# Down projections of a two-layer decoder trunk: four of eleven pairs of k-tiles by seven block products with summed blocks in place of eight products

## The chip, the cores and the metric

The kernel runs on one core of one Trainium2 chip. The metric is the device time of one execution in microseconds: the median of three runs is 652.33 us (651.77 to 652.62). The profile is one more execution, taken with the hardware profiler, and has its own time.

The engines are named as the profile names them: PE multiplies matrices, PEld is PE's loading of the stationary operand, DVE is the vector engine (VectorE), ACT the scalar engine (ScalarE), POOL is GpSimd, and SP issues the DMA transfers of the weights.

## The reference

The input is 256 tokens of width 1024. Two layers follow each other, each a mixer and a feed-forward part; the change is in the feed-forward parts alone:

```python
D_MODEL, SEQ, DEPTH = 1024, 256, 2
D_FF = -(-8 * D_MODEL // (3 * 256)) * 256        # 2816

def rmsnorm(x, g):
    y = x * lax.rsqrt(jnp.mean(x * x, axis=-1, keepdims=True) + NORM_EPS)
    return y * g

def swiglu(h, w_gate, w_up, w_down):
    return (jax.nn.silu(h @ w_gate) * (h @ w_up)) @ w_down

for layer in range(DEPTH):
    x = x + mixer(rmsnorm(x, norm_mix[layer]))   # even: two attention groups, odd: sparse attention
    x = x + swiglu(rmsnorm(x, norm_ffn[layer]), ffn_w_gate[layer], ffn_w_up[layer], ffn_w_down[layer])
return rmsnorm(x, norm_final)
```

All of it is float32. The down projection is the product of the units, `silu(gate) * up`, a matrix of 256 tokens by 2816, with `w_down`, 2816 by 1024.

## The kernel before

**How a float32 product is made.** Each operand is split in two: a `hi` part, the value rounded to the matrix engine's `float32r` type (a copy on ACT), and a `lo` part, the rest (a subtraction on DVE). A product is then three matmuls into one bank of PSUM (function `mm3`, lines 363 to 365): hi by hi, hi by lo, lo by hi. The gate and up projections (lines 503 and 505) have a form of their own, in which one matmul of 512 columns takes both parts of the activations and one of 256 columns takes the low part of the weights.

**The weight stream.** The class `Weights` walks a list of weight tiles in the order of their use. A tile is 128 partitions by up to 1024 columns, 512 KB. `load` (line 95) issues its transfer on SP into one of four raw buffers, `prepare` makes `w_hi` on ACT (line 111) and `w_lo` on DVE (line 114), each in a ring of seven buffers. `next` hands out the next tile and first prepares the tiles up to six ahead. So there are three releases: a raw buffer is free for the next transfer when DVE has made its `w_lo`; a `w_hi` or `w_lo` buffer is free for the tile seven further on when PE has done the last matmul that reads it.

**The order on an engine.** Each engine executes its own list strictly in order and waits at an instruction until its semaphores are reached; PE alone loads stationary operands ahead. A scheduler made the lists when the program was built, from the order in which the code records operations; nothing is reordered on the chip.

**The feed-forward part** (function `ffn`) has two stages.

- *Gate and up*, eleven chunks of 256 of the 2816 columns. A chunk takes two weight tiles for gate (banks `ps_g`, two of the four banks with the tag `mm`) and two for up (banks `ps_u`, the two banks with the tag `s`). Then come, for each of its two groups of 128 columns, an ACT copy and a DVE sum out of the bank (lines 514 and 518), a scaling, the Silu and the product `hn` (lines 515, 516, 519), a tile of 128 units by 256 tokens. `split` (line 247) makes its `hT_hi` on ACT and `hT_lo` on DVE. The units stand with the units on the partitions, and so are the stationary operand of the next stage.
- *Down*, function `residual`. The 2816 units are 22 k-tiles of 128, so eleven pairs. The 1024 columns of the result are two halves `h` of 512, the 256 tokens two halves `t` of 128: four blocks, each with one of the four `mm` banks, `ps_out`. For each k-tile, one weight tile (128 units by 1024 columns) is taken, and each of the four blocks gets its three matmuls: 12 matmuls of 512 columns. The last three k-tiles are held back and taken block by block, so that a block is complete early: DVE adds it, times the token's `rs`, to the residual stream `x` (line 448), and the next norm begins (line 281), or in the last layer the final norm (lines 330 to 353).

## Time and profile before

| what | value |
|---|---|
| median of 3 runs | 652.33 us (651.77 to 652.62) |
| the profiled execution, its own time | 652.22 us |
| its span, first to last instruction | 650.4 us |
| granted TensorE clock, mean | 0.997 |
| PE busy | 638.9 us, 98% of the span |
| PEld busy | 537.5 us, 83% |
| DVE busy | 478.9 us, 74% |
| ACT busy | 403.0 us, 62% |
| DMA of the weights | 107.79 MB on SP's queue, 49.3% of 16 engines' span |
| down stage of the first layer, first to last matmul's start | 261.34 to 322.43 us |
| down stage of the second layer, first to last matmul's start | 583.33 to 643.19 us |

How to read it: times are counted in us from the start of the span. The profiled execution's own time is 1.8 us longer than its span. A row of a timeline has the start, the length, the engine, the line of the kernel, the operation with its output and inputs, and in brackets how long the engine was idle before and what ended that. A row of the groups has, after the bar, the busy time in us and the mean length of one instruction in ns, and then the idle time before the group. Matmuls of one row follow each other before the previous one has ended, so the distance of two starts, not the length of one, is what a matmul takes.

### The profile page before, as it was taken

Reading aid. Unit: us, or ns where it says so; the run is one execution under the profiler, and the core shown is the slowest. Engines: PE = TensorE matmul, PEld = TensorE weight load, DVE = VectorE, ACT = ScalarE, POOL = GpSimd, SP = SyncE. Lnnn points to the kernel's source line nnn. Section 1 sums busy time; section 2 is a strip of 40 time slices with the busy share of each in tenths; the row PEclk is TensorE's granted clock in tenths of the full one; section 3 lists DMA queues with packets and bytes.
Section 4 is the critical chain, followed back from the end, with each engine's and each line's share of the span. In section 5 each row is a group of like instructions: output and inputs, shape, how many; then the busy total and the mean of one; then the engine's idle time right before and its main releaser. Section 6 shows DMA issues by size and latency. Waiting matters only on the chain.

```text
span 650.4 us, 10025 instructions
## 1 busy us (share of the span) xinstructions
PE 638.9 (98%) x3521; PEld 537.5 (83%) x3521; DVE 478.9 (74%) x1116; ACT 403.0 (62%) x809; POOL 11.0 (2%) x26
## 2 busy tenths in 40 slices
PE   8999999999999999999999999999999999999995
PEld 5978888888888888888888877776888888888884
DVE  6999976678867677544589889797887777765424
ACT  6685748558665665433377597787676665564314
POOL 2000000100000000000000000000000000000000
PEclk9999999999999999999999999999999999999998
DMA  8834354218755655564186511402286555556501
GB/s 302 295 128 153 98 172 154 97 53 287 244 194 194 193 187 190 183 194 151 49 328 234 188 67 56 171 34 93 85 283 234 190 187 187 183 185 210 191 14 66
DMA packets 31729, 109.02 MB, mean 168 GB/s; under 512 B 3648, under 2 KB 3904, under 8 KB 31424
## 3 DMA queue, kind: packets, MB, share of 16 engines
q1 hardware_dynamic: 31104, 107.79, 49.3%
q10 hardware_dynamic: 576, 0.59, 0.3%
q8 instruction: 28, 0.46, 0.3%
q14 instruction: 21, 0.17, 0.1%
HBM read 107.32 MB, written 1.05 MB: 167 GB/s over the span
## 4 chain that ended last, share of the span: by engine, by line
PE 88%; ACT 4%; DVE 4%; DMA 2%; issue 1%; SPq 0%; POOL 0%; ACTq 0%; DVEq 0%
PE ps_g L503 12%; PE ps_u L503 12%; PE ps_out L364 8%; PE ps_out L365 8%; PE ps_out L363 8%; PE ps_u L505 6%; PE ps_g L505 6%; PE ps_in L364 5%; PE ps_in L365 5%; PE ps_in L363 5%; PE pt_p L998 2%; PE ps_o L1014 2%; PE ps_s L978 1%; DVE w_lo L114 1%; ACT e L466 1%
## 5 line engine op out<-in xcount | busy, mean ns | idle before, releaser
L114 DVE TENSOR_TENSOR w_lo<-w_raw,w_hi 128x1024 fp32r<-128x1024 f32 (+5 forms) x200 | 231.5, 1179 | 112.6 <-ACT w_hi L111 67.7
L111 ACT ACTIVATE w_hi<-w_raw 128x1024 fp32r<-128x1024 f32 (+5 forms) x200 | 203.4, 1025 | 135.5 <-PE ps_out L365 53.4
L503 PE MATMUL ps_u<-aW,w_hi 128*128 128x512 f32 x352 | 84.9, 391 | 0.0
L503 PE MATMUL ps_g<-aW,w_hi 128*128 128x512 f32 x352 | 84.5, 391 | 0.0
L364 PE MATMUL ps_in<-w_lo,aW 128*128 128x512 f32 (+5 forms) x208 | 77.2, 371 | 0.1
L363 PE MATMUL ps_in<-w_hi,aW 128*128 128x512 f32 (+5 forms) x208 | 76.8, 370 | 0.1
L365 PE MATMUL ps_in<-w_hi,aW 128*128 128x512 f32 (+5 forms) x208 | 75.5, 363 | 0.0
L503 PEld LDWEIGHTS ps_g<-aW,w_hi 128*128 128x128 f32 x352 | 64.6, 188 | 13.1 <-DVE aW L247 0.7
L503 PEld LDWEIGHTS ps_u<-aW,w_hi 128*128 128x128 f32 x352 | 64.4, 188 | 12.2
L364 PE MATMUL ps_out<-w_lo,hT_hi 128*128 128x512 f32 (+1 forms) x176 | 68.3, 388 | 0.0
L363 PE MATMUL ps_out<-w_hi,hT_hi 128*128 128x512 f32 (+1 forms) x176 | 68.3, 388 | 0.0
L365 PE MATMUL ps_out<-w_hi,hT_lo 128*128 128x512 f32 (+1 forms) x176 | 68.3, 388 | 0.0
L505 PEld LDWEIGHTS ps_u<-aW,w_lo 128*128 128x128 f32 x352 | 45.4, 191 | 1.9
L505 PEld LDWEIGHTS ps_g<-aW,w_lo 128*128 128x128 f32 x352 | 45.4, 191 | 1.9
L505 PE MATMUL ps_g<-aW,w_lo 128*128 128x256 f32 x352 | 46.0, 283 | 0.0
L505 PE MATMUL ps_u<-aW,w_lo 128*128 128x256 f32 x352 | 46.0, 283 | 0.0
L466 ACT ACTIVATE e<-e,bias 128x128 f32<-128x128 f32 (+1 forms) x96 | 42.4, 446 | 1.3 <-DVE bias L465 0.9
L364 PEld LDWEIGHTS ps_in<-w_lo,aW 128*128 128x128 f32 x208 | 39.3, 189 | 4.6 <-issue 0.5
L363 PEld LDWEIGHTS ps_in<-w_hi,aW 128*128 128x128 f32 x208 | 39.2, 189 | 4.7 <-ACT w_hi L111 0.3
L365 PEld LDWEIGHTS ps_in<-w_hi,aW 128*128 128x128 f32 x208 | 39.2, 188 | 4.6 <-issue 0.5
L365 PEld LDWEIGHTS ps_out<-w_hi,hT_lo 128*128 128x128 f32 x176 | 33.1, 188 | 6.8
L363 PEld LDWEIGHTS ps_out<-w_hi,hT_hi 128*128 128x128 f32 x176 | 33.1, 188 | 6.7
(237 smaller groups left out, 874.7 us busy)
## 6 DMA issues: line engine op xcount, KB each, us to landing
w_raw<-in_w SPq DMA_DIRECT2D x176, 512.0 KB, 3.8
w_raw<-in_w SPq DMA_DIRECT2D x8, 384.0 KB, 4.5
gain<-in_vec SPq DMA_DIRECT2D x4, 512.0 KB, 5.4
cw<-in_cw SPq DMA_DIRECT2D x2, 1024.0 KB, 7.0
w_raw<-in_w SPq DMA_DIRECT2D x4, 416.0 KB, 5.2
w_raw<-in_w SPq DMA_DIRECT2D x4, 328.0 KB, 5.1
w_raw<-in_w SPq DMA_DIRECT2D x4, 304.0 KB, 2.7
x<-in_x SPq DMA_DIRECT2D x4, 256.0 KB, 5.0
```

Of the source, the lines that this page charges most:

```text
L111: act = nc.scalar.activation(hi[:, :n], raw[:, :n], AF.Copy)
L114: sub = nc.vector.tensor_sub(lo[:, :n], raw[:, :n], hi[:, :n])
L363: TE.matmul(ps, act[0][:, k], wh, start=start, stop=False, skip_group_check=skip),
L364: TE.matmul(ps, act[0][:, k], wl, start=False, stop=False, skip_group_check=skip),
L365: TE.matmul(ps, act[1][:, k], wh, start=False, stop=stop, skip_group_check=skip),
L466: return low, A.activation(e, e, AF.Exp, scale=-1.0, bias=bias, accum_out=den)
L503: TE.matmul(dst[f], wt[0][:, i, f * P : (f + 1) * P], wide[:, k].rearrange("p z q -> p (z q)"), start=k == 0, stop=False)
L505: TE.matmul(dst[f][:, :T], wt[1][:, i, f * P : (f + 1) * P], wide[:, k, 0], start=False, stop=k == KD - 1)
L978: mmi = TE.matmul(sb[:, i], qS[t][:, h], kz[:, par, :, :ns], start=z == 0, stop=z == 1)
L998: TE.transpose(pt[:, i, b, st], e[:, i, b, st * P : (st + 1) * P], ident)
L1014: pin(TE.matmul(ob[64 * par : 64 * par + 64], vv[:, st, c : c + 64], pTs[par][:, b, st].rearrange("p j c -> p (j c)"), start=False, stop=l ...
```

## The change

The down projection of a pair of k-tiles is a product of 2 by 2 blocks: units of k-tile 2g and 2g+1, each for the token halves 0 and 1 (a11 and a21 of the first k-tile, a12 and a22 of the second), and weights with the two column halves (b11 and b12 of the first k-tile, b21 and b22 of the second). It takes eight block products, and each is three matmuls. The change computes it for the pairs 1, 3, 5 and 7 with seven:

- sums of units: S1 = a21 + a22, S2 = S1 - a11, S3 = a11 - a21, S4 = a12 - S2
- sums of weights: T1 = b12 - b11, T2 = b22 - T1, T3 = b22 - b12, T4 = b21 - T2
- products: P1 = a11 b11, P2 = a12 b21, P3 = S4 b22, P4 = a22 T4, P5 = S1 T1, P6 = S2 T2, P7 = S3 T3
- results: block (0,0) is P1 + P2, block (0,1) is P1 + P6 + P5 + P3, block (1,0) is P1 + P6 + P7 + P4, block (1,1) is P1 + P6 + P7 + P5

P2, P3 and P4 go to the banks `ps_out` of their blocks. P1, P5, P6 and P7 are accumulated over the four pairs in four banks more (`ps_p1`, `ps_p6` with the tag `s`, `ps_p5`, `ps_p7` with the tag `tp`), and are combined once, after the last of the four pairs: an ACT copy and six DVE instructions, which add them to `x`.

The sums of weights are made on DVE in float32 from two raw tiles (`pair`), and split like any weight (`halves`). Seven blocks of 512 columns are split for a pair, T1 to T4, b11, b21 and b22, where four were; b12 is not needed by itself. The split of the sums stands in two pairs of buffers, and for the second and later pairs it is recorded after the matmuls of the pair before (`close`). The sums of units are made on DVE behind the second `hn` of the chunk (`seven_units`) and are split too; the units of a22 and a12 are split as before, a21 is not split by itself. The other seven pairs, and all that stands outside the feed-forward part, have the same instructions in the same order as before.

```diff
--- before.py
+++ after.py
@@ -30,6 +30,7 @@
 OD_CHUNKS = [304, 256, 512, 512, 512, 512]
 FF_CHUNKS = [256] * 11
 WCOLS = 1024
+FAST = (1, 3, 5, 7)
 
 
 def in_tiles(chunks):
...
@@ -100,6 +104,11 @@
         nc = self.tc.nc
         while len(self.ready) < min(upto, len(self.queue)):
             i = len(self.ready)
+            if i in self.pairs:
+                if i + 2 > upto:
+                    break
+                self.pair(i)
+                continue
             self.load(i + 1)
             raw = self.raw[i]
             self.raw[i] = None
@@ -115,6 +124,58 @@
                 self.parts.append((act, sub))
             self.ready.append((hi[:, :n].rearrange("p (k c) -> p k c", k=kk), lo[:, :n].rearrange("p (k c) -> p k c", k=kk)))
 
+    def halves(self, hi, lo, src):
+        act = self.tc.nc.scalar.activation(hi, src, AF.Copy)
+        return act, self.tc.nc.vector.tensor_sub(lo, src, hi)
+
+    def pair(self, i):
+
+        V = self.tc.nc.vector
+        self.load(i + 2)
+        a, b = self.raw[i : i + 2]
+        self.raw[i : i + 2] = [None] * 2
+        sums = [self.sums.tile([P, WCOLS], F32, tag="ts", bufs=2, name="w_sum") for _ in range(2)]
+        h = slice(0, 512), slice(512, 1024)
+        got = {}
+        for n, (names, src) in enumerate((((("b11",), a), (("b21", "b22"), b)))):
+            hi = self.pool.tile([P, WCOLS], F32R, tag="hi", bufs=self.bufs[1], name="w_hi")
+            lo = self.pool.tile([P, WCOLS], F32R, tag="lo", bufs=self.bufs[1], name="w_lo")
+            c = slice(0, 512 * len(names))
+            self.parts.append(self.halves(hi[:, c], lo[:, c], src[:, c]))
+            for j, name in enumerate(names):
+                got[name] = (hi[:, h[j]], lo[:, h[j]])
+        V.tensor_sub(sums[0][:, h[0]], a[:, h[1]], a[:, h[0]])
+        V.tensor_sub(sums[0][:, h[1]], b[:, h[1]], a[:, h[1]])
+        V.tensor_sub(sums[1][:, h[0]], b[:, h[1]], sums[0][:, h[0]])
+        V.tensor_sub(sums[1][:, h[1]], b[:, h[0]], sums[1][:, h[0]])
+        self.ready += [got, None]
+        if self.open is None:
+            self.open = (got, sums)
+            self.close()
+        else:
+            self.open = (got, sums)
+
+    def close(self):
+
+        if self.open:
+            got, sums = self.open
+            for j, names in enumerate((("t1", "t3"), ("t2", "t4"))):
+                hi = self.sums.tile([P, WCOLS], F32R, tag="thi", bufs=2, name="w_shi")
+                lo = self.sums.tile([P, WCOLS], F32R, tag="tlo", bufs=2, name="w_slo")
+                self.halves(hi, lo, sums[j])
+                for n, name in enumerate(names):
+                    c = slice(512 * n, 512 * n + 512)
+                    got[name] = (hi[:, c], lo[:, c])
+            self.open = ()
+
...
@@ -379,7 +440,7 @@
                 nm.finish()
         return ps
 
-    def residual(act, nk, tail, nxt, rs=None, amid=None, gate=(), hold=False):
+    def residual(act, nk, tail, nxt, rs=None, amid=None, fast=(), seven=None, gate=(), hold=False):
 
         ps = [[mm_bank("ps_out") for _ in range(2)] for _ in range(NT)]
         inorder = amid is not None and not hold
@@ -389,11 +450,17 @@
             skip = isinstance(nxt, Final) and (t, h) == (NT - 1, 1)
             return mm3(ps[t][h], act[t], k, wt[0][:, 0, c], wt[1][:, 0, c], k == 0, k == nk - 1 - skip * tail, skip)
 
-        for k in range(nk - tail):
+        k = 0
+        while k < nk - tail:
+            if k in fast:
+                seven(ps, k)
+                k += 2
+                continue
             wt = W.next()
             for t in range(NT):
                 for h in range(2):
                     one(t, h, k, wt)
+            k += 1
         last = [W.next(hold=tail) for _ in range(tail)]
         if amid and not hold:
             order = [(t, h, 0, tail) for t, h in ((0, 0), (0, 1), (1, 0), (1, 1))]
@@ -469,8 +536,80 @@
         wide, rs = nm.wide, nm.rs
         nxt = Final() if goff == V_FIN else Norm(goff)
         with tc.tile_pool(name="ffn", bufs=1, side="left", reuse_waits="tile") as fp:
-            hh = fp.tile([P, KF, T], F32R, tag="hh", name="hT_hi")
-            hl = fp.tile([P, KF, T], F32R, tag="hl", name="hT_lo")
+            at, sums_at, o = {}, {}, 0
+            for k in range(0, KF, 2):
+                if k // 2 in FAST:
+                    at[0, k], at[0, k + 1], at[1, k + 1], sums_at[k] = o, o + P, o + 2 * P, o + 3 * P
+                    o += 7 * P
+                else:
+                    for i in range(2):
+                        for t in range(NT):
+                            at[t, k + i] = o + (NT * i + t) * P
+                    o += 4 * P
+            hh = fp.tile([P, o], F32R, tag="hh", name="hT_hi")
+            hl = fp.tile([P, o], F32R, tag="hl", name="hT_lo")
+            W.sums = fp
+            W.open = None
+            down = W.used + 2 * KD // ff_kk(FF_CHUNKS[0]) * len(FF_CHUNKS)
+            W.pairs = {down + 2 * g for g in FAST}
+
...
+            def seven_units(k, hn):
+
+                ss = fp.tile([P, 4, P], F32, tag="ss", name="h_sum")
+                a11, a21, a12, a22 = (hn[i][:, t * P : (t + 1) * P] for i in range(2) for t in range(NT))
+                V.tensor_add(ss[:, 0], a21, a22)
+                V.tensor_sub(ss[:, 1], ss[:, 0], a11)
+                V.tensor_sub(ss[:, 2], a11, a21)
+                V.tensor_sub(ss[:, 3], a12, ss[:, 1])
+                o = at[0, k]
+                split(hh[:, o : o + P], hl[:, o : o + P], a11)
+                split(hh[:, o + P : o + 3 * P], hl[:, o + P : o + 3 * P], hn[1])
+                o = sums_at[k]
+                split(hh[:, o : o + 4 * P], hl[:, o : o + 4 * P], ss.rearrange("p s q -> p (s q)"))
+
+            made = {}
+
+            def seven(ps, k):
+
+                if not made:
+                    for n in (5, 7):
+                        made[n] = t_bank(f"ps_p{n}")
+                    for n in (6, 1):
+                        made[n] = s_bank(f"ps_p{n}")
+                first, last = k == 2 * FAST[0], k == 2 * FAST[-1]
+                w = W.both()
+                o = sums_at[k]
+                terms = (
+                    (made[5], o, "t1", first, last),
+                    (made[7], o + 2 * P, "t3", first, last),
+                    (made[6], o + P, "t2", first, last),
+                    (ps[1][0], at[1, k + 1], "t4", False, False),
+                    (made[1], at[0, k], "b11", first, last),
+                    (ps[0][0], at[0, k + 1], "b21", False, False),
+                    (ps[0][1], o + 3 * P, "b22", False, False),
+                )
+                for dst, o, name, start, stop in terms:
+                    u = [z[:, o : o + P].unsqueeze(1) for z in (hh, hl)]
+                    mm3(dst, u, 0, *w[name], start, stop)
+                W.close()
+                if last:
+                    ua = W.sums.tile([P, 2, 512], F32, tag="ts", bufs=2, name="c_sum")
+                    ub = W.sums.tile([P, 2, 512], F32, tag="ts", bufs=2, name="c_sum")
+                    evac(ua[:, 0], made[6])
+                    V.tensor_add(ua[:, 0], made[1], ua[:, 0])
+                    V.scalar_tensor_tensor(xs[0][:, :512], made[1], rs[0], xs[0][:, :512], op0=ALU.mult, op1=ALU.add)
+                    V.tensor_add(ua[:, 1], made[5], ua[:, 0])
+                    V.scalar_tensor_tensor(xs[0][:, 512:], ua[:, 1], rs[0], xs[0][:, 512:], op0=ALU.mult, op1=ALU.add)
+                    V.tensor_add(ub, made[7].unsqueeze(1).broadcast_to([P, 2, 512]), ua)
+                    V.scalar_tensor_tensor(xs[1], ub.rearrange("p a c -> p (a c)"), rs[1], xs[1], op0=ALU.mult, op1=ALU.add)
 
 
...
@@ -517,12 +657,17 @@
                     evac(hn, up[f][:, T:])
                     V.tensor_add(hn, up[f][:, :T], hn)
                     V.tensor_mul(hn, hn, sg)
-                    split(hh[:, f0 + f], hl[:, f0 + f], hn)
+                    hns.append(hn)
+                    if f0 // nf not in FAST:
+                        o = at[0, f0 + f]
+                        split(hh[:, o : o + T], hl[:, o : o + T], hn)
+                    elif f:
+                        seven_units(f0, hns)
                 f0 += nf
                 if f0 == 3 * nf:
                     gain(goff)
-            hT = [[z[:, :, t * P : (t + 1) * P] for z in (hh, hl)] for t in range(NT)]
-            residual(hT, KF, 3, nxt, rs)
+            hT = [[Units(z, t) for z in (hh, hl)] for t in range(NT)]
+            residual(hT, KF, 3, nxt, rs, fast={2 * g for g in FAST}, seven=seven)
         return nxt
 
 
```

The order on the engines is shown at three places of the first layer's feed-forward part; the second layer's reads the same.

PE, down stage. `ps_out_2894` and `ps_out_2895` are two of the four blocks' banks, `w_hi_2830` and `w_lo_2831` the split weight tile of one k-tile, `hT` the units. Before, each k-tile has such rows for four banks:

```order
L363 MATMUL ps_out_2894<-w_hi_2830,hT_hi_1601 128x512
L364 MATMUL ps_out_2894<-w_lo_2831,hT_hi_1601 128x512
L365 MATMUL ps_out_2894<-w_hi_2830,hT_lo_1602 128x512
L363 MATMUL ps_out_2895<-w_hi_2830,hT_hi_1601 128x512
L364 MATMUL ps_out_2895<-w_lo_2831,hT_hi_1601 128x512
L365 MATMUL ps_out_2895<-w_hi_2830,hT_lo_1602 128x512
```

With the change, the middle of the first such pair (`w_shi_2834` and `w_slo_2835` are the split of T2 and T4, `w_hi_2818` of b11, `w_hi_2822` of b21 and b22):

```order
L424 MATMUL ps_p6_2984<-w_shi_2834,hT_hi_1601 128x512
L425 MATMUL ps_p6_2984<-w_slo_2835,hT_hi_1601 128x512
L426 MATMUL ps_p6_2984<-w_shi_2834,hT_lo_1602 128x512
L424 MATMUL ps_out_2938<-w_shi_2834,hT_hi_1601 128x512
L425 MATMUL ps_out_2938<-w_slo_2835,hT_hi_1601 128x512
L426 MATMUL ps_out_2938<-w_shi_2834,hT_lo_1602 128x512
L424 MATMUL ps_p1_2985<-w_hi_2818,hT_hi_1601 128x512
L425 MATMUL ps_p1_2985<-w_lo_2819,hT_hi_1601 128x512
L426 MATMUL ps_p1_2985<-w_hi_2818,hT_lo_1602 128x512
L424 MATMUL ps_out_2936<-w_hi_2822,hT_hi_1601 128x512
L425 MATMUL ps_out_2936<-w_lo_2823,hT_hi_1601 128x512
L426 MATMUL ps_out_2936<-w_hi_2822,hT_lo_1602 128x512
```

Ahead of these rows stand the three matmuls of P5 and the three of P7, behind them the three of P3: 21 matmuls of the same form, where 24 stood.

DVE, the end of gate and up (from the gate sums of the tenth chunk to those of the eleventh and last), before:

```order
L514 TENSOR_TENSOR sg<-ps_g,sg 128x256 x2
L515 TENSOR_TENSOR sg<-sg,rB 128x256 x2
L114 TENSOR_TENSOR w_lo<-w_raw,w_hi 128x1024 x2
L518 TENSOR_TENSOR hn<-ps_u,hn 128x256 x2
L519 TENSOR_TENSOR hn<-hn,sg 128x256 x2
L247 TENSOR_TENSOR hT_lo<-hn,hT_hi 128x256 x2
L114 TENSOR_TENSOR w_lo<-w_raw,w_hi 128x1024 x2
L514 TENSOR_TENSOR sg<-ps_g,sg 128x256 x2
```

and with the change, from the row behind the same scalings by `rB`:

```order
L147 TENSOR_TENSOR w_sum<-w_raw 128x512
L148 TENSOR_TENSOR w_sum<-w_raw 128x512
L149 TENSOR_TENSOR w_sum<-w_raw,w_sum 128x512
L123 TENSOR_TENSOR w_lo<-w_raw,w_hi 128x1024
L658 TENSOR_TENSOR hn<-ps_u,hn 128x256 x2
L659 TENSOR_TENSOR hn<-hn,sg 128x256 x2
L129 TENSOR_TENSOR w_lo<-w_raw,w_hi 128x512
L308 TENSOR_TENSOR hT_lo<-hn,hT_hi 128x256
L150 TENSOR_TENSOR w_sum<-w_raw,w_sum 128x512
```

Behind them stand the other `hT_lo`, a `w_slo` of 1024, a `w_lo` of 1024, a second `w_slo`, a `w_lo`, and then the two sums `sg<-ps_g,sg` of the last chunk (line 654). So the four sums of the first pair and the two splits of sums stand ahead of the instructions that read the last gate banks.

DVE, down stage. Before, it holds only `w_lo` of 128x1024, one for each k-tile (a row of 14 equal ones). With the change, one round of a plain pair and a summed pair reads:

```order
L129 TENSOR_TENSOR w_slo<-w_sum,w_shi 128x1024
L147 TENSOR_TENSOR w_sum<-w_raw 128x512
L129 TENSOR_TENSOR w_slo<-w_sum,w_shi 128x1024
L123 TENSOR_TENSOR w_lo<-w_raw,w_hi 128x1024
L129 TENSOR_TENSOR w_lo<-w_raw,w_hi 128x512
L148 TENSOR_TENSOR w_sum<-w_raw 128x512
L149 TENSOR_TENSOR w_sum<-w_raw,w_sum 128x512
L150 TENSOR_TENSOR w_sum<-w_raw,w_sum 128x512
L129 TENSOR_TENSOR w_lo<-w_raw,w_hi 128x1024
L123 TENSOR_TENSOR w_lo<-w_raw,w_hi 128x1024
```

Four instructions of 1024 columns have become ten: five of 1024 and five of 512.

More of the change, by code (lines that the diff above doesn't have):

```diff
@@ L89, in __init__ @@
         self.later = 0
+        self.pairs = {}
+        self.sums = None
+        self.open = None
     def load(self, upto):
@@ L116, in prepare, with both @@
             self.ready.append((hi[:, :n].rearrange("p (k c) -> p k c", k=kk), lo[:, :n].rearrange("p (k c) -> p k c", k=kk)))
+    def halves(self, hi, lo, src):
[37 more added lines that the diff above has]
+            self.open = ()
+    def both(self):
+        i = self.used
+        self.used += 2
+        self.prepare(i + 2 + self.ahead)
+        got = self.ready[i]
+        self.ready[i] = None
+        return got
     def next(self, hold=1):
@@ new lines, in ffn, with __init__, __getitem__ @@
+            hh = fp.tile([P, o], F32R, tag="hh", name="hT_hi")
[4 more added lines that the diff above has]
+            W.pairs = {down + 2 * g for g in FAST}
+            class Units:
+                def __init__(self, z, t):
+                    self.z, self.t = z, t
+                def __getitem__(self, c):
+                    o = at[self.t, c[1]]
+                    return self.z[:, o : o + P]
@@ L509, in ffn @@
                         spread()
+                hns = []
                 for f in range(nf):
```

## The prediction

> **What bounds the kernel now.** First the page's busy times and its chain of waits:
>
> ```profile
> PE 638.9 (98%) x3521; PEld 537.5 (83%) x3521; DVE 478.9 (74%) x1116; ACT 403.0 (62%) x809; POOL 11.0 (2%) x26
> PE 88%; ACT 4%; DVE 4%; DMA 2%; issue 1%; SPq 0%; POOL 0%; ACTq 0%; DVEq 0%
> PE ps_g L503 12%; PE ps_u L503 12%; PE ps_out L364 8%; PE ps_out L365 8%; PE ps_out L363 8%; PE ps_u L505 6%; PE ps_g L505 6%; PE ps_in L364 5%; PE ps_in L365 5%; PE ps_in L363 5%; PE pt_p L998 2%; PE ps_o L1014 2%; PE ps_s L978 1%; DVE w_lo L114 1%; ACT e L466 1%
> ```
>
> PE makes 88% of the chain, and the three lines of `ps_out` together 24%. So a matmul less in a place where PE never waits is worth its whole spacing. Then the table of windows, because the shares are means over stages: the last gate and up chunk, and the middle of both down stages (window, its length, busy time of PE, PEld, DVE, ACT, POOL; clock; DMA share; GB/s).
>
> ```profile
> 249.90:261.30 11.40, 11.40 (x68) 10.11 (x68) 8.41 (x15) 6.79 (x12) 0.00 (x0) 1.00 0.55 186
> 282.00:302.00 20.00, 20.00 (x90) 16.57 (x89) 9.55 (x8) 7.43 (x7) 0.00 (x0) 1.00 0.56 181
> 603.00:623.00 20.00, 20.00 (x90) 16.56 (x89) 8.84 (x8) 8.14 (x8) 0.00 (x0) 1.00 0.46 158
> ```
>
> PE is busy all the time at full clock; DVE has 10 of 20 us free in the down stage, and 3 of 11.4 in a gate and up chunk. Last, PE's timeline for the spacing, and DVE's for who waits for whom (start, length, instruction, idle time before it):
>
> ```profile
> 266.81 0.39 PE L363 MATMUL ps_out<-w_hi,hT_hi 128*128 128x512 f32 x1
> ...
> 269.53 0.39 PE L363 MATMUL ps_out<-w_hi,hT_hi 128*128 128x512 f32 x1
> ```
>
> ```profile
> 270.83 1.23 DVE L114 TENSOR_TENSOR w_lo<-w_raw,w_hi 128x1024 fp32r<-128x1024 f32 x1 [1.49 <-ACT w_hi L111]
> 273.55 1.22 DVE L114 TENSOR_TENSOR w_lo<-w_raw,w_hi 128x1024 fp32r<-128x1024 f32 x1 [1.49 <-ACT w_hi L111]
> ```
>
> The two matmuls are twelve apart, one k-tile: 2.72 us, or 0.2267 us for each. DVE does one `w_lo` in the same 2.72 us and then waits 1.49 us for `w_hi`, which itself waits for PE to give a buffer of the ring of seven back. The splitting is thus held back by PE, not PE by the splitting.
>
> **The change part by part.** *Removed: matmuls.* Each of four pairs loses one block product of three matmuls, in two layers: 4 x 2 x 3 = 24, all of the 512-column form. 24 x 0.2267 = 5.44 us. All the others keep their form, and each still has a stationary load of its own, so I take the spacing as unchanged. The bound below is the nearest cheaper row, line 505 with 256 columns,
>
> ```profile
> 259.59 1.91 PE ps_u L505 x16
> ```
>
> 0.119 us each, which would make it 2.9 us. I take 5.44, the row of the same form and place.
>
> The Trainium skill, "TensorE: Matmul & The Clock Gate", section "Back-to-back issue gap", gives a stream of load and matmul about 131 ns for each matmul of 512 columns. By that the 24 would be worth 3.1 us and the forecast 649.2; this trace has 227 ns and does not agree.
>
> *Added on DVE in the down stage.* The durations, from the groups by form:
>
> ```profile
> L114 DVE TENSOR_TENSOR w_lo<-w_raw,w_hi 128x1024 fp32r<-128x1024 f32 x176 | 211.0, 1221 | 100.9 <-ACT w_hi L111 56.0 <-issue 34.1 <-PE ps_g L505 10.5
> L114 DVE TENSOR_TENSOR w_lo<-w_raw,w_hi 128x512 fp32r<-128x512 f32 x4 | 2.6, 684 | 0.0
> L281 DVE TENSOR_TENSOR xg<-x,gain 128x512 f32<-128x512 f32 x12 | 8.3, 690 | 0.3
> L448 DVE SCALAR_TENSOR_TENSOR x<-ps_out,rs,x 128x512 f32<-128x512 f32 x7 | 5.2, 749 | 13.4 <-PE ps_out L365 13.2
> L111 ACT ACTIVATE w_hi<-w_raw 128x1024 fp32r<-128x1024 f32 x176 | 185.3, 1059 | 121.6 <-PE ps_out L365 45.7 <-PE ps_u L503 23.4 <-PE ps_g L503 21.5
> ```
>
> A round is one plain pair and one summed pair: PE needs (24 + 21) x 0.2267 = 10.20 us. DVE's ten instructions are five of 1024 and five of 512: 5 x 1.221 + 0.684 + 4 x 0.690 = 9.55 us, 94% of the round, against 4 x 1.221 = 4.88 us before. ACT has five and a half splits of 1024, 5.5 x 1.059 = 5.8 us. It fits, but with 0.65 us to spare: the cover is thin in rate. Rows for two instructions in a row show that starts overlap:
>
> ```profile
> 255.02 2.36 DVE L114 TENSOR_TENSOR w_lo<-w_raw,w_hi 128x1024 fp32r<-128x1024 f32 x2 [0.61 <-PE ps_g L505]
> 257.30 0.75 DVE L514 TENSOR_TENSOR sg<-ps_g,sg 128x256 f32<-128x256 f32 x2
> ...
> 262.92 0.75 DVE L518 TENSOR_TENSOR hn<-ps_u,hn 128x256 f32<-128x256 f32 x2
> ```
>
> Two of 1024 take 2.36, not 2.44, so 9.55 is on the high side. The new wait: the split sums have buffers for one pair only. The first half is free when PE has done P5 and P7 of the pair before, and is wanted 15 + 24 = 39 matmuls later, 8.84 us. In it ACT needs 1.06, and then DVE 1.22, each behind at most one plain split (1.06 and 1.22): 4.6 us. Four us remain, and the same distance holds for the second half, with one sum of 0.69 between. I take 0 for this, and 0 to 1 us a pair as its bounds.
>
> *Added at the end of gate and up.* Here the order stands against the change: sums and splits of the first pair are ahead of `sg<-ps_g`, which frees the banks of block (1,0) and (1,1), wanted by the seventh matmul of the stage:
>
> ```profile
> 262.73 0.39 PE L363 MATMUL ps_out<-w_hi,hT_hi 128*128 128x512 f32 x1
> ...
> L95 SPq DMA_DIRECT2D w_raw<-in_w x7: 328/328/328, 245.2 to 261.9; - x7
> DMA to landing us min/median/max: 3.5/3.6/4.4
> ...
> 246.83 0.75 DVE L515 TENSOR_TENSOR sg<-sg,rB 128x256 f32<-128x256 f32 x2
> ```
>
> Before, the first of the two `sg` is done by 257.72 and the bank has 5 us of slack. With the change, the first sum follows the tenth chunk's scaling, the row at 246.83, and runs from 247.58 to 248.27; the second needs the pair's second raw tile, whose transfer goes out at 245.2 and lands at 248.8. Then two sums to 250.2, `w_lo` to 251.4, two pairs of 256 columns (1.5) to 252.9, the split of b11 to 253.6, `hT_lo` 0.42, a sum 0.69 and `hT_lo` 0.42 to 255.1, and four of 1024 to 260.0; the first `sg` is done at 260.4. That leaves 2.3 us of the slack. Value 0; upper bound 2 us a layer, if the transfer is as late as several in a queue. The banks of `ps_u`, wanted by P6 31 matmuls into the stage, at 268.1, were freed by the row at 262.92; with one sum and the later queue it is 264.2, and 4 us are left.
>
> *Added in gate and up*, four chunks a layer: four sums of 128 columns and splits of 128, 256 and 512 in place of two of 256. The nearest rows:
>
> ```profile
> L458 DVE SCALAR_TENSOR_TENSOR rope_b<-ps_in,rs,con 128x128 f32<-128x128 f32 x12 | 3.7, 342 | 0.0
> L247 DVE TENSOR_TENSOR hT_lo<-hn,hT_hi 128x256 fp32r<-128x256 f32 x44 | 17.1, 422 | 7.5 <-ACT hT_hi L247 7.4
> ```
>
> 5 x 0.34 + 0.42 + 0.69 - 2 x 0.42 = 2.0 us, in a chunk with 3.0 us free. The weights are prepared up to seven tiles ahead, so a DVE late by 2 us delays no matmul: 0. Without that cover it would be 2 us x 8 chunks.
>
> *Added after the last summed pair:* one ACT copy and six DVE instructions; an estimate from the rows above is 0.69 + 0.75 + 0.69 + 0.75 + 1.22 + 1.28 (the last as 749 plus half of 1.06) = 5.4 us. They must end before the first addition of `ps_out` to `x`, three plain k-tiles and nine matmuls later: 45 x 0.2267 = 10.2 us. In the first layer five splits for the next tiles stand among them (1.22 and four of about 0.8, 4.4 us), 9.8 in all, most of them early. Value 0; if 1 us late, the other three blocks' matmuls, 27 of them, hide it.
>
> *DMA:* the same transfers; 0.
>
> **The sum.** 652.22 (the profiled execution, span 650.4) - 5.44 = 646.78. The median of the runs is 0.11 higher, so the forecast for the median is 652.33 - 5.44 = 646.9.
>
> **The rivals.**
>
> *PE stalls at the entry or at a summed pair* (0.14). For it: the queue at the end of gate and up uses over half of a 5 us slack, and in-order DVE waits at raw tiles and at ACT. Against it: 2.3 us and 4 us are left. 1 to 2 us a layer: 648.9 to 650.9.
>
> *A removed matmul is worth less than its spacing* (0.02): 0.119 us, 649.5. Against it: the even spacing over whole stages.
>
> *The weights' transfers become the bound* (0.03): a round moves four tiles in 10.2 instead of 10.88 us. For it: SP issues only when DVE gives a raw buffer back, and a summed pair holds two of four longer. Against it:
>
> ```profile
> w_raw<-in_w SPq DMA_DIRECT2D x176, 512.0 KB, 3.8
> GB/s 302 295 128 153 98 172 154 97 53 287 244 194 194 193 187 190 183 194 151 49 328 234 188 67 56 171 34 93 85 283 234 190 187 187 183 185 210 191 14 66
> ```
>
> 190 GB/s here, 328 elsewhere. It would give the gain back: 652.3.
>
> *VectorE becomes the bound of the down stage* (0.07), the case on the slower side. Place: the three rounds from the first summed pair to the last. It begins when DVE's round passes 10.20 us, 7% over my 9.55; it costs more than the stage gains, 2.72 us, when three rounds exceed that by 2.72 plus the 4 us of lead, at 12.4 us a round. That takes sums at the price of 1024 columns (4 x 0.53 = 2.1 more) and one unhidden wait of 1.5 us for `w_hi`, as in the rows above: 13.15 us, three rounds 8.9 over, 4.9 after the lead, 2.2 lost a layer: 656.7. For it: the strict order and 94%. Against it: the 512-column rows, which are near half of 1221, and ACT with 4 us free a round.
>
> *The change does not save matmuls* is left out: PE's order has 21 where 24 stood.
>
> **How the numbers follow.** 0.74 for the forecast, with a range of its own of 646.2 to 647.8. No change can be told apart from one within 0.2%, 1.3 us, so faster means below 651.0: 0.74 + 0.14 + 0.02 = 0.90; same 0.03; slower 0.07. The range reaches into the first rival: 645.9 to 649.6.
>
> **What would show it.** Right: in the down stages 24 matmul starts fewer at 0.227 us, the summed pairs 4.76 us long, stages of 58.4 us for 61.1 and 57.1 for 59.9; DVE's busy share of the middle near 0.9, PE still 20.00 of 20. Wrong: idle time of PE or PEld at `ps_p5` or `ps_p6` released by `w_slo` or `w_shi`, at the stage's seventh matmul released by `sg`, or a spacing other than 0.227.

## The result, and the profile after

| kernel | median (lowest to highest), us | ratio to before, 95% interval |
|---|---|---|
| before | 652.62 (651.77 to 653.01), 5 runs | |
| changed | 647.27 (646.89 to 647.34), 5 runs | 0.9919 [0.9905, 0.9934] |

The change saves 5.35 us. The forecast was 646.9 us, with 5.44 us saved. (The median before is now of five runs, 652.62 us, where three gave 652.33.) The profiled execution took 646.89 us, 5.33 less than the one before; its span is 645.1 us.

The page of the changed kernel, its busy times and its chain of waits:

```profile
PE 633.6 (98%) x3497; PEld 533.0 (83%) x3497; DVE 531.0 (82%) x1216; ACT 420.5 (65%) x835; POOL 11.0 (2%) x26
PE 88%; ACT 4%; DVE 3%; DMA 2%; issue 1%; POOL 0%; SPq 0%; ACTq 0%
```

PE has 24 matmuls less and 5.3 us less busy time, and its share of the chain is the same 88%. DVE has 100 instructions and 52.1 us of work more (531.0 against 478.9), nearly ten times what was saved, and DVE's share of the chain did not grow. All that work lies beside PE. The windows of the changed kernel say where: a gate and up chunk in which unit sums are made, the last chunk, the first two rounds of the first down stage, its middle, and the start of the second (window, its length, busy time of PE, PEld, DVE, ACT, POOL; clock; DMA share; GB/s).

```profile
227.10:238.50 11.40, 11.40 (x69) 10.11 (x68) 9.48 (x20) 7.43 (x14) 0.00 (x0) 1.00 0.57 169
...
249.90:261.30 11.40, 11.40 (x68) 10.11 (x68) 11.40 (x20) 7.83 (x14) 0.00 (x0) 1.00 0.54 160
...
269.50:279.70 10.20, 10.20 (x46) 8.45 (x46) 9.02 (x10) 5.81 (x6) 0.00 (x0) 1.00 0.70 213
279.70:289.90 10.20, 10.20 (x46) 8.45 (x46) 9.05 (x10) 5.81 (x6) 0.00 (x0) 1.00 0.65 202
...
282.00:302.00 20.00, 20.00 (x90) 16.57 (x89) 14.90 (x16) 10.56 (x11) 0.00 (x0) 1.00 0.62 195
580.70:603.00 22.30, 22.30 (x101) 18.46 (x100) 20.31 (x27) 13.03 (x16) 0.00 (x0) 1.00 0.61 191
```

In every one PE is busy for the whole window, at full clock. DVE is not idle at all in the last chunk, has 9.0 of 10.2 us to do in a round, and 20.3 of 22.3 us at the start of the second layer's stage. PE's timeline has the lengths (start, length, instruction):

```profile
261.35 0.40 PE L424 MATMUL ps_out<-w_hi,hT_hi 128*128 128x512 f32 x1
...
266.82 0.39 PE L424 MATMUL ps_p<-w_shi,hT_hi 128*128 128x512 f32 x1
...
271.58 0.39 PE L424 MATMUL ps_out<-w_hi,hT_hi 128*128 128x512 f32 x1
...
319.71 0.40 PE L426 MATMUL ps_out<-w_hi,hT_lo 128*128 128x512 f32 x1
...
580.74 0.40 PE L424 MATMUL ps_out<-w_hi,hT_hi 128*128 128x512 f32 x1
```

The first summed pair lasts from 266.82 to 271.58, 4.76 us for 21 matmuls, 0.2267 us each. The first layer's stage lasts from 261.35 to 319.71: 58.4 us, where it was 61.1. The second layer's stage begins 2.59 us earlier than before (580.74 against 583.33), which is about what the first one gained, and the rest is gained in the second: it lasts to 637.88, 57.1 us, where it was 59.9.

### The profile page after: what moved, and what is told of

It is laid out like the page before. It is cut to its first block, busy times and chain, and to the rows that moved or that the text cites. A ratio compares the mean times of both kernels' runs of the same rounds, so it can differ in the third digit from the quotient of the medians.

```text
span 645.1 us, 10109 instructions
## 1 busy us (share of the span) xinstructions
PE 633.6 (98%) x3497; PEld 533.0 (83%) x3497; DVE 531.0 (82%) x1216; ACT 420.5 (65%) x835; POOL 11.0 (2%) x26
## 4 chain that ended last, share of the span: by engine, by line
PE 88%; ACT 4%; DVE 3%; DMA 2%; issue 1%; POOL 0%; SPq 0%; ACTq 0%
PE ps_g L642 12%; PE ps_u L642 12%; PE ps_g L644 7%; PE ps_u L644 7%; PE ps_out L425 6%; PE ps_out L426 6%; PE ps_out L424 6%; PE ps_in L425 5%; PE ps_in L424 5%; PE ps_in L426 5%; PE pt_p L1143 2%; PE ps_o L1159 2%; DMA w_raw<-in_w 2%; PE ps_s L1123 1%; PE ps_p L425 1%; PE ps_p L424 1%
## 5 line engine op out<-in xcount | busy, mean ns | idle before, releaser
L123 DVE TENSOR_TENSOR w_lo<-w_raw,w_hi 128x1024 fp32r<-128x1024 f32 (+5 forms) x184 | 212.9, 1176 | 61.7 <-ACT w_hi L120 32.7
L120 ACT ACTIVATE w_hi<-w_raw 128x1024 fp32r<-128x1024 f32 (+5 forms) x184 | 186.4, 1020 | 103.0 <-PE ps_out L426 23.3
L425 PE MATMUL ps_out<-w_lo,hT_hi 128*128 128x512 f32 (+1 forms) x128 | 49.7, 388 | 0.0
L426 PE MATMUL ps_out<-w_hi,hT_lo 128*128 128x512 f32 (+1 forms) x128 | 49.7, 388 | 0.0
L424 PE MATMUL ps_out<-w_hi,hT_hi 128*128 128x512 f32 (+1 forms) x128 | 49.6, 388 | 0.0
L424 PEld LDWEIGHTS ps_out<-w_hi,hT_hi 128*128 128x128 f32 x128 | 24.1, 188 | 4.8
L532 DVE CUSTOM_DVE_ANT_0 e<-ps_s,con 128x128 f32<-128x128 f32 (+1 forms) x80 | 25.2, 349 | 3.4 <-PE ps_s L1123 1.8
```

What stands on the lines that cost most here:

```text
L120: act = nc.scalar.activation(hi[:, :n], raw[:, :n], AF.Copy)
L123: sub = nc.vector.tensor_sub(lo[:, :n], raw[:, :n], hi[:, :n])
L424: TE.matmul(ps, act[0][:, k], wh, start=start, stop=False, skip_group_check=skip),
L425: TE.matmul(ps, act[0][:, k], wl, start=False, stop=False, skip_group_check=skip),
L426: TE.matmul(ps, act[1][:, k], wh, start=False, stop=stop, skip_group_check=skip),
L532: low = V.tensor_tensor_reduce(e, s, m, -scale, 3e38, ALU.add, ALU.min, bias)
```

## The experiments

The theory is that of the prediction: a removed matmul is worth its spacing, 0.2267 us, and everything added is hidden as long as DVE's round stays below PE's. The rivals to be told apart: that the removed matmuls are worth more or less than that and the added work costs or returns the difference; and that the price at which DVE becomes the bound is not where the prediction put it. Time and ratio of all nine runs:

| run | what it is | us | before, same chip | ratio, 95% interval |
|---|---|---|---|---|
| e1_drop24 | before, 24 matmuls left out | 647.22 | 652.61 | 0.9924 [0.9912, 0.9937] |
| e2_eight | all the added work, no matmul saved | 652.96 | 652.61 | 1.0003 [0.9994, 1.0012] |
| e3_twopairs | two summed pairs | 650.03 | 652.61 | 0.9965 [0.9953, 0.9977] |
| e4_poolsums | weight sums on GpSimd | 648.02 | 652.61 | 0.9933 [0.9921, 0.9946] |
| e5_dve2 | two sums of 1024 columns more a pair | 649.97 | 652.21 | 0.9967 [0.9954, 0.9980] |
| e6_dve4 | four of them | 663.39 | 652.21 | 1.0175 [1.0157, 1.0193] |
| e7_five | five summed pairs | 645.23 | 652.21 | 0.9891 [0.9878, 0.9904] |
| e8_after_again | the change again | 646.38 | 652.01 | 0.9910 [0.9895, 0.9925] |
| e9_five_again | e7_five again | 645.01 | 652.01 | 0.9886 [0.9870, 0.9903] |

**e1_drop24: the gain without the work.** The kernel before, with eight k-tiles of block (1,1) left out, four a layer. This leaves out part of the result.

```diff
--- before.py, in the loop of residual
+++ e1_drop24
                 for h in range(2):
+                    if rs is not None and (t, h) == (1, 1) and k in (3, 7, 11, 15):
+                        continue
                     one(t, h, k, wt)
```

> The kernel before, with block (1,1) of the k-tiles 3, 7, 11 and 15 left out of both down projections: 24 matmuls of 512 columns less, nothing added (this part of the result is left out). Theory: a matmul removed from a full PE is worth its spacing, 24 x 0.2267 = 5.44 us, so 5.4 us below the kernel before, and within 0.5 us of the changed kernel. Rival (a removed matmul is worth less than its spacing): 2.9 us below. If the added work of the change costs something, this kernel is faster than the changed one by that much.

Measured: 647.22 us, 5.39 less than before, and 0.9924 [0.9912, 0.9937] against 0.9919 [0.9905, 0.9934] of the change. So 24 matmuls of this form are worth 5.39 / 24 = 0.225 us each, and leaving them out with nothing added gives the same as the whole change. With a matmul at 0.119 us the run would have come out at 649.8.

**e2_eight: the work without the gain.** The changed kernel with one block product too many, added to block (1,1), so that a summed pair has 24 matmuls again; the eighth product is not part of the result.

```diff
--- after.py, in seven
+++ e2_eight
                     (ps[1][0], at[1, k + 1], "t4", False, False),
+                    (ps[1][1], at[1, k + 1], "b22", False, False),
...
```

> The changed kernel with an eighth block product in each of the four pairs (a22 b22 once more, into block (1,1), so that the result has a product too many): all the sums, splits and the combination of the change, and the 24 matmuls back. Theory (all that is added is hidden): the time of the kernel before, within 1 us, and down stages of 61.1 and 59.9 us as before. Rival (something that is added costs time that the seven products give back): above the kernel before by that time, 1 to 4 us for the stalls at the entry or at the pairs.

Measured: 652.96 us, 1.0003 [0.9994, 1.0012]. All sums, splits, buffers, banks and the combination together cost between 0.4 us of gain and 0.8 us of loss. Its first down stage lasts 61.1 us again (261.96 to 323.04). The profile of this run has DVE near the busy time of the change (531.0 us) and PE near that of before (638.9):

```profile
PE 640.5 (98%) x3521; PEld 539.1 (83%) x3521; DVE 531.7 (82%) x1216; ACT 420.1 (65%) x835; POOL 11.0 (2%) x26
```

A round is 10.88 us of PE here, not 10.20, so the cover is thicker than in the change; that the thinner cover holds too is what e1 says.

**e3_twopairs: half of it.** Only the pairs 1 and 3 are summed.

```diff
-FAST = (1, 3, 5, 7)
+FAST = (1, 3)
```

> The changed kernel with the pairs 1 and 3 alone by seven products. Theory: 12 matmuls less than the kernel before, 12 x 0.2267 = 2.72 us below it, half the gain of the change. Rival (a fixed cost for the combination or for the first pair, paid once a layer): less than half, since two pairs carry the same fixed cost as four; with a fixed cost of f in all the gain is 2.72 - f here and 5.44 - f with four pairs.

Measured: 650.03 us, 2.58 saved where 12 matmuls make 2.72. The gain goes with the number of matmuls; there is no fixed cost of having summed pairs at all that would show here (0.14 us is inside the interval).

**e4_poolsums: the weight sums on another engine.** If DVE's load cost anything, taking the four sums of each pair away from it should give it back.

```diff
-        V.tensor_sub(sums[0][:, h[0]], a[:, h[1]], a[:, h[0]])
+        self.tc.nc.gpsimd.tensor_sub(sums[0][:, h[0]], a[:, h[1]], a[:, h[0]])
...
```

(and so for the other three).

> The changed kernel with the four sums of weights of each pair made on GpSimd in place of VectorE. VectorE is relieved of 16 x 2 instructions of 0.69 us, 22 us of busy time. Theory (VectorE's work in the down stage is hidden already): the time of the changed kernel, within 0.7 us, if the four sums take GpSimd less than about 10 us a round. No trace here shows such a GpSimd instruction, so its price is open: at 0.7 us each nothing moves, at over 2.5 us each a round is bound by GpSimd and the time grows by three times the excess a layer. Rival (VectorE's load costs some of the gain): faster than the changed kernel by up to 0.5 us.

Measured: 648.02 us, 0.9933 [0.9921, 0.9946]: no gain over the change (647.27 us), whose interval overlaps. But DVE was not relieved. Its windows in the first down stage of e4_poolsums, and the groups of the operations concerned:

```profile
273.00:283.00 10.00, 10.00 (x45) 8.26 (x45) 10.00 (x6) 5.24 (x7) 8.31 (x4) 1.00 0.67 201
283.00:293.00 10.00, 10.00 (x46) 8.27 (x45) 10.00 (x7) 5.28 (x6) 8.09 (x4) 1.00 0.66 200
```

```profile
L147 POOL TENSOR_TENSOR w_sum<-w_raw 128x512 f32<-128x512 f32 x8 | 15.6, 1945 | 230.9 <-DMA w_raw<-in_w 111.7 <-PE ps_u L642 106.4 <-DVE w_slo L129 12.8
L129 DVE TENSOR_TENSOR w_lo<-w_raw,w_hi 128x1024 fp32r<-128x1024 f32 x8 | 14.1, 1764 | 0.0
L129 DVE TENSOR_TENSOR w_lo<-w_raw,w_hi 128x512 fp32r<-128x512 f32 x8 | 12.0, 1503 | 0.0
```

The same two groups on DVE in the changed kernel:

```profile
L129 DVE TENSOR_TENSOR w_lo<-w_raw,w_hi 128x1024 fp32r<-128x1024 f32 x8 | 9.8, 1221 | 0.0
...
L129 DVE TENSOR_TENSOR w_lo<-w_raw,w_hi 128x512 fp32r<-128x512 f32 x8 | 5.5, 687 | 0.0
```

DVE is busy all of the time with six or seven instructions in 10 us, where it had ten in 10.2 us and was busy for 9.0. The same subtractions that take 1221 and 687 ns on average in the changed kernel take 1764 and 1503 here. So this run says nothing of what a relieved DVE would bring. It does say something of the lead. Two rows of e4_poolsums' DVE timeline, a round apart:

```profile
272.86 2.35 DVE L129 TENSOR_TENSOR w_slo<-w_sum,w_shi 128x1024 fp32r<-128x1024 f32 x2
...
283.54 2.35 DVE L129 TENSOR_TENSOR w_slo<-w_sum,w_shi 128x1024 fp32r<-128x1024 f32 x2
```

DVE's round is 10.68 us, longer than PE's 10.20, and PE is still busy for all of the time: three rounds fall back by 1.4 us, and the lead covers that.

**e5_dve2 and e6_dve4: more work for DVE, until it shows.** Sums of 1024 columns whose result is written over, ahead of the real ones.

```diff
--- after.py, in pair
+++ e5_dve2 (e6_dve4 has 4)
                 got[name] = (hi[:, h[j]], lo[:, h[j]])
+        for _ in range(2):
+            V.tensor_sub(sums[0], a, b)
         V.tensor_sub(sums[0][:, h[0]], a[:, h[1]], a[:, h[0]])
```

> The changed kernel with two more subtractions of 128x1024 on VectorE for each of the four pairs (made of the two raw tiles into the buffer of the first sums, and overwritten). The scheduler puts them ahead of the pair's sums. Theory, with the prediction's price of 9.55 us a round and a lead of 4 us: 9.55 + 2 x 1.22 = 12.0 us against 10.20, three rounds 5.4 us over, 1.4 us a layer after the lead, 650.1 us. Theory, with the profile of the changed kernel, where a round has about 8.9 us of VectorE's work by the starts of its instructions (269.5 to 279.7, 1.3 us of it waiting) and the split of the sums is ready 6 us ahead: 8.9 + 2 x 1.14 = 11.2 us, three rounds 3 us over, less than the lead: 647.3 us, no change. Rival (no rate limit, the waits between ScalarE and VectorE decide): no change at four more either.

> As above with four more subtractions of 128x1024 a pair. With the prediction's price and lead: 9.55 + 4.88 = 14.4 us a round, three rounds 12.7 over, 8.7 us a layer after 4 us of lead: 664.7 us. With the changed kernel's profile: 8.9 + 4.6 = 13.5 us, three rounds 9.9 us over, 3.6 to 4 us a layer after 6 us of lead: 654 to 655 us, with PE waiting at the matmuls of P5 and P6 for the split of sums. Either way VectorE's rate is then the bound, and slower than the kernel before (652.6). Rival (the added work is hidden whatever it is): 647.3 us.

Measured: e5_dve2 649.97 us, 0.9967 [0.9954, 0.9980]; e6_dve4 663.39 us, 1.0175 [1.0157, 1.0193]. The prediction's price (three rounds over 10.20 us, less 4 us of lead, in each layer) says about 650 from a round of 9.55 + 2 x 1.22 = 11.99 (647.3 + 2 x (3 x 1.79 - 4)), and 664.7 from 14.43. Both are met to within 1.4 us, but in part by luck: that sum has a round of 9.55 us and a lead of 4 us, and the changed kernel has about 9.0 and 6.3 (next section). With its own figures the two expectations said 647.3 us and 654 to 655 us, and both were missed, by 2.7 and 8 us. Nor is the loss of e5_dve2 spread as the sum has it, 1.4 us in each layer. The last matmul of its first down stage starts at 322.04 us against 319.71 in the change, that of the second at 640.90 against 637.88: 2.3 us were lost by the end of the first stage (0.3 of it before the stage began), and 0.7 after it.

The low price of e5_dve2 and the steep rise to e6_dve4 fit a lead that is used up once. In the windows of e5_dve2, two rounds of 11.4 us, PE loses its full count in the second, and the waits of its weight loads have a new row, 2.7 us in six waits (us in total, times, longest):

```profile
269.80:281.20 11.40, 11.40 (x52) 9.45 (x51) 11.09 (x13) 5.73 (x6) 0.00 (x0) 1.00 0.59 184
281.20:292.60 11.40, 10.86 (x49) 8.66 (x48) 11.13 (x13) 5.72 (x6) 0.00 (x0) 1.00 0.56 184
```

```profile
PEld ps_p L426 <- ACT w_shi L128: 2.7, 6, 1.0
...
PE ps_out L426 <- DVE sg L656: 0.5, 1, 0.5
```

The first row is the one that the prediction named for a wrong forecast: the split of a sum that comes too late. The second, a wait of PE itself, is at the other place that it named, the entry of the stage, where PE waits for `sg`. Neither is in the changed kernel. In e6_dve4 it is there in seven waits, and the plain splits come late as well:

```profile
PEld ps_p L426 <- ACT w_shi L128: 3.1, 7, 0.8
...
PEld ps_out L427 <- DVE w_lo L123: 1.8, 3, 0.8
```

But most of what e6_dve4 loses does not stand in the rounds. The last matmul of its first down stage starts 3.5 us later than in the change (323.18 against 319.71), the first of the second layer's stage 9.8 us later (590.58 against 580.74): over 6 us are lost between the two. PE's longest wait there is for the next norm, 2.5 us for DVE's `xg` right behind the stage.

One caution: the added sums also moved the rest of the lists, since they are made anew for each program. In e5_dve2 both halves of a pair's split go together, right behind the last of that pair's sums. The split at 276.74, in the rows below, is for the pair that PE begins at 278.10, so nothing of the lead of 6.3 us is left at the second pair. PE's list has changed too: in e6_dve4 the last matmul with a split sum starts at 316.4, where it does at 299.9 in the change. The two runs show how little more DVE can take, not the effect of a rate alone.

```profile
276.74 2.50 DVE L129 TENSOR_TENSOR w_slo<-w_sum,w_shi 128x1024 fp32r<-128x1024 f32 x2
...
288.16 2.50 DVE L129 TENSOR_TENSOR w_slo<-w_sum,w_shi 128x1024 fp32r<-128x1024 f32 x2
```

From 276.74 to 288.16 it is 11.42 us: the round now lasts about as long as DVE's twelve instructions, which keep it busy for 11.1 us. In e6_dve4 the same two rows are 13.79 us apart (283.49 and 297.28).

**e7_five: one pair more.** If the work is hidden and only a plain pair between two summed ones is needed, then five pairs, 0, 2, 4, 6 and 8, have the same rounds and save 30 matmuls. The first pair now opens the stage, so its products start the banks; the sums of units take the place of a buffer that stands idle then.

```diff
-FAST = (1, 3, 5, 7)
+FAST = (0, 2, 4, 6, 8)
...
-                ss = fp.tile([P, 4, P], F32, tag="ss", name="h_sum")
+                ss = nat("h_sum").rearrange("p (s q) -> p s q", s=4)
...
-                    (ps[1][0], at[1, k + 1], "t4", False, False),
+                    (ps[1][0], at[1, k + 1], "t4", k == 0, False),
...
-                    (ps[0][0], at[0, k + 1], "b21", False, False),
-                    (ps[0][1], o + 3 * P, "b22", False, False),
+                    (ps[0][0], at[0, k + 1], "b21", k == 0, False),
+                    (ps[0][1], o + 3 * P, "b22", k == 0, False),
```

(In `one`, block (1,1) starts its bank at k = 2.)

> The changed kernel with five pairs, 0, 2, 4, 6 and 8, by seven products; the sums of units stand in a buffer of the norm that is idle there, for room, and the first matmul of a block's bank sets it where pair 0 comes first. Theory: 6 matmuls less than the changed kernel, 6 x 0.2267 = 1.36 us: 645.9 us; the spacing of the pairs, and so VectorE's rate, is the same. Rivals: the combination stands only 21 matmuls, 4.8 us, ahead of the first addition to x in place of 10.2, and has 9.8 us of VectorE's queue in the first layer, so up to 5 us late there, of which 6 us of matmuls of the other blocks hide most: 0 to 3 us of loss, 645.9 to 649; or P6 waits as the seventh matmul of the stage for the banks of the last up chunk, 0 to 2 us a layer.

Measured: 645.23 us, 0.9891 [0.9878, 0.9904]: 6.98 us saved, for 30 x 0.2267 = 6.80. Windows of e7_five, the start of the first down stage and its middle:

```profile
261.30:282.00 20.70, 20.70 (x93) 17.08 (x92) 20.60 (x30) 12.37 (x18) 0.00 (x0) 1.00 0.65 197
282.00:302.00 20.00, 20.00 (x90) 16.57 (x89) 16.52 (x17) 11.74 (x12) 0.00 (x0) 1.00 0.66 200
```

DVE has 0.1 us left in the first 20.7, and PE waits nowhere in either. The cover is now used up at the other end too. The rows of e7_five's DVE timeline, the first and the last of the combination, and the first addition of `ps_out`:

```profile
305.51 0.69 DVE L607 TENSOR_TENSOR c_sum<-ps_p,c_sum 128x512 f32<-128x512 f32 x1 [1.88 <-PE ps_p L426]
...
311.26 1.28 DVE L612 SCALAR_TENSOR_TENSOR x<-c_sum,rs,x 128x1024 f32<-128x1024 f32 x1
312.46 0.75 DVE L515 SCALAR_TENSOR_TENSOR x<-ps_out,rs,x 128x512 f32<-128x512 f32 x1
```

The combination ends when the first addition begins, and PE then waits once behind the stage:

```profile
PE ps_in L426 <- DVE aW L308: 0.5, 1, 0.5
```

**e8_after_again and e9_five_again: the two on one chip.** No edit; the change and e7_five side by side.

> The changed kernel once more, beside the one with five pairs on the same chip. Theory: 5.4 us below the kernel before, ratio 0.992.

> The kernel with five pairs once more. Theory: 1.36 us below the changed kernel of the same call, ratio to the kernel before 0.9897 (30 matmuls, 6.8 us). If it is 2 us below, as the first measurement had it against the changed kernel of another call, something beside the six matmuls gains.

Measured: 646.38 and 645.01 us, 1.37 apart, where six matmuls make 1.36. The two intervals, [0.9895, 0.9925] and [0.9870, 0.9903], overlap a little, and the earlier pair of results, 0.9919 and 0.9891, lies the same way. e7_five is the fastest kernel of this study.

## Why the prediction was right, point by point

**The removed matmuls: 24 x 0.2267 = 5.44 us.** Right. e1_drop24 measures 5.39 us for this term alone, and the change 5.35. The rival of a cheaper matmul falls with it. By the figure of the Trainium skill, "TensorE: Matmul & The Clock Gate", section "Back-to-back issue gap" (about 131 ns for a matmul of 512 columns), an estimate for e1_drop24 is 649.5 us. It measured 647.22, which does not agree.

**DVE's round: 9.55 of 10.20 us, "on the high side".** Right in kind, 0.53 us too high: the windows above have 9.02 and 9.05. The prediction added up single lengths; instructions in a row start before the one ahead has ended (two of 1024 columns, at 254.41 and 255.55, take 1.22 us each and start 1.14 us apart), and that is the difference. It had the price of a sum right: 0.69 us from the 512-column rows, and 0.69 in the rows below. DVE's share of the middle of the stage is 14.90 of 20, 0.75, less than the 0.9 that was named, since that window reaches past the last sums; in the rounds it is 0.88.

**The split sums: 4 us of lead left.** It was more. Rows of the changed kernel's DVE timeline:

```profile
269.47 1.23 DVE L129 TENSOR_TENSOR w_slo<-w_sum,w_shi 128x1024 fp32r<-128x1024 f32 x1
270.73 0.69 DVE L147 TENSOR_TENSOR w_sum<-w_raw 128x512 f32<-128x512 f32 x1
...
279.72 1.23 DVE L129 TENSOR_TENSOR w_slo<-w_sum,w_shi 128x1024 fp32r<-128x1024 f32 x1
```

The split that ends at 270.70 is read from 277.02 on, where the second summed pair begins on PE:

```profile
277.02 0.39 PE L424 MATMUL ps_p<-w_shi,hT_hi 128*128 128x512 f32 x1
```

That is 6.3 us, and no wait of PE or of its weight loads at `ps_p` stands in the changed kernel's list of waits.

**The entry to the stage: first `sg` done at 260.4, 2.3 us left.** The mechanism was right, the size 1 us too strict. The sums stand ahead of `sg`, and the second one waits for the raw tile as told:

```profile
247.50 0.69 DVE L147 TENSOR_TENSOR w_sum<-w_raw 128x512 f32<-128x512 f32 x1
248.86 0.69 DVE L148 TENSOR_TENSOR w_sum<-w_raw 128x512 f32<-128x512 f32 x1 [0.67 <-DMA w_raw<-in_w]
...
258.95 0.76 DVE L654 TENSOR_TENSOR sg<-ps_g,sg 128x256 f32<-128x256 f32 x2
...
262.02 0.75 DVE L658 TENSOR_TENSOR hn<-ps_u,hn 128x256 f32<-128x256 f32 x2
```

Rows of its PE timeline, the matmuls that want the banks:

```profile
262.74 0.39 PE L424 MATMUL ps_out<-w_hi,hT_hi 128*128 128x512 f32 x1
...
268.18 0.39 PE L424 MATMUL ps_p<-w_shi,hT_hi 128*128 128x512 f32 x1
```

The tile landed at 248.86 (248.8 predicted). The first of the two `sg` is done at about 259.3 (half of the pair's 0.76 us on), and the bank is wanted by the stage's seventh matmul at 262.74: 3.4 us are left. The working again counted single lengths. The banks of `ps_u` are free by 262.8, wanted at 268.18: 5.4 us left where 4 were told.

**Unit sums: 2.0 us a chunk.** DVE has 9.48 us to do from 227.10 to 238.50, where the kernel before has 8.27 in the same window:

```profile
227.10:238.50 11.40, 11.40 (x69) 10.11 (x68) 8.27 (x15) 6.98 (x13) 0.00 (x0) 1.00 0.58 194
```

It is 1.21 us more. The nearest row, 342 ns for 128 columns, was an operation of another kind; the sums take 0.29 us each, and overlap:

```profile
230.86 0.29 DVE L570 TENSOR_TENSOR h_sum<-hn 128x128 f32<-128x128 f32 x1
```

**The combination: done in 9.8 of 10.2 us.** Rows of the changed kernel:

```profile
301.09 0.69 DVE L607 TENSOR_TENSOR c_sum<-ps_p,c_sum 128x512 f32<-128x512 f32 x1 [1.10 <-PE ps_p L426]
...
307.28 1.28 DVE L612 SCALAR_TENSOR_TENSOR x<-c_sum,rs,x 128x1024 f32<-128x1024 f32 x1
...
312.58 0.75 DVE L515 SCALAR_TENSOR_TENSOR x<-ps_out,rs,x 128x512 f32<-128x512 f32 x1 [0.50 <-PE ps_out L426]
```

From 301.09 to 308.56 it is 7.5 us, and 4 us are left before the first addition, which waits for PE and not for DVE.

**The transfers: 0.** 195 GB/s in the middle of the stage, against 181 before, and PE has no wait in either down stage.

**The rivals.** PE's stall at the entry did not come, with 3.4 us left where the prediction had 2.3. VectorE as the bound did not come at 9.02 us a round. That it comes with more work is shown by e5_dve2 and e6_dve4, and the price is near the one named: 656.7 us for a round of 13.15 us, and e6_dve4 has 663.39 with one of 13.8. The place is only in part the named one, since e6_dve4 loses most of its time behind the first stage; and in the sum the round was 0.5 us too long and the lead 2 us too short, both on the strict side. What e2_eight adds is that the sum of all terms put at nothing is nothing, to within 0.8 us, at a round of 10.88 us.

## What to carry to other kernels

Where PE is busy in every window of a stage, count what a removed matmul is worth from the distance of two starts in that stage, and then spend the other engines' idle time freely: here 52 us of VectorE work bought 5.35 us of PE. What has to be counted is the load for each round of the stage and the lead at its entry and exit, not the share of busy time over the span; two more instructions of 1.22 us a round took away over half of the gain, and four turned it into a loss. Moving work to a second engine is no relief before the trace shows that the first engine's instructions keep their length.

## What the runs showed of the hardware

GpSimd and VectorE held each other up in e4_poolsums. Rows of its GpSimd timeline, the second sum of the second pair and the first two of the third, and rows of its VectorE timeline beside them:

```profile
265.55 1.62 POOL L148 TENSOR_TENSOR w_sum<-w_raw 128x512 f32<-128x512 f32 x1 [5.49 <-ACT hn L281]
267.13 1.48 POOL L149 TENSOR_TENSOR w_sum<-w_raw,w_sum 128x512 f32<-128x512 f32 x1
...
274.15 2.21 POOL L147 TENSOR_TENSOR w_sum<-w_raw 128x512 f32<-128x512 f32 x1 [4.10 <-DVE w_slo L129]
276.33 2.27 POOL L148 TENSOR_TENSOR w_sum<-w_raw 128x512 f32<-128x512 f32 x1
```

```profile
265.94 0.74 DVE L658 TENSOR_TENSOR hn<-ps_u,hn 128x256 f32<-128x256 f32 x2
266.61 2.29 DVE L659 TENSOR_TENSOR hn<-hn,sg 128x256 f32<-128x256 f32 x2
...
271.72 1.22 DVE L123 TENSOR_TENSOR w_lo<-w_raw,w_hi 128x1024 fp32r<-128x1024 f32 x1
...
275.13 2.32 DVE L123 TENSOR_TENSOR w_lo<-w_raw,w_hi 128x1024 fp32r<-128x1024 f32 x1
```

The split at 271.72, with GpSimd idle, took 1.22 us; the same instruction at 275.13, with GpSimd at work, took 2.32. At 265.94 VectorE read PSUM for one of its two inputs while GpSimd worked, and took its 0.74 us for two; the next two instructions, of the same size and with both inputs in SBUF, took 2.29. The second layer has the same pair at 585.27 and 585.93, 0.74 and 2.67 us. So the delay is not GpSimd's work as such, but goes with two inputs in SBUF on VectorE. The Trainium skill, "SBUF — State Buffer", section "Who interferes with whom", has a rule of this kind: VectorE's second SBUF port is shared with GpSimd, and one of the two is locked out while the other uses it. The trace agrees: the split of 275.13 ends 1.09 us after the sum of 274.15 has ended (277.45 and 276.36), about what it takes alone. A sum of 512 columns took GpSimd 1.29 to 2.28 us, and 1.30 at 249.70, where VectorE stood idle for nearly all of it; on VectorE it took 0.69. So even alone GpSimd would not be the faster place.
